# One decode step of a hybrid decoder: the sample tokens' experts move from the dense pass to gathered rows

## The chip, the cores and the metric

The kernel runs on one core of a Trainium2 chip. The metric is the device time of one execution in microseconds; the median of three runs is used. The engines are TensorE (PE, with its weight loads as PEld), VectorE (DVE), ScalarE (ACT), GpSimd (POOL) and SyncE (SP); 16 DMA engines serve all of them.

## What is computed

One layer works on 1024 prompt tokens and on 64 sample tokens (8 sequences of 8), each of 1024 channels. A state-space branch and a dilated attention branch are mixed, and a retrieval step over 16384 single-neuron experts follows. Only that last step is touched by the change:

```python
def block(xb):                       # 128 tokens
    q = einsum('td,dq->tq', xb, w_qp).reshape(TOKEN_BLOCK, PEER_HEADS, 2, PEER_HALF)
    s = einsum('thpe,hpke->thpk', q, sub_keys)
    sv, si = lax.top_k(s, PEER_TOPK)             # 16 of 128 keys, twice
    ...                                          # the 16 best pairs of each of 8 heads
    eidx = ...                                   # (128 tokens, 128 experts)
    gate = softmax(best, axis=-1).reshape(TOKEN_BLOCK, PEER_HEADS * PEER_TOPK)
    ue = jnp.take(u_tab, eidx, axis=0)
    act = gelu(einsum('td,tkd->tk', xb, ue))
    ve = jnp.take(v_tab, eidx, axis=0)
    return einsum('tk,tkd->td', gate * act, ve)
```

Each token so needs 128 of the 16384 rows of `u_tab` and of `v_tab`; a row has 1024 float32 values, 4 KB.

## The kernel before

The prompt is worked in two halves of 512 tokens. The 64 samples are projected with the first half (576 tokens there) and mixed with the second (576 tokens there). All large products are done in float32r in three parts (high times high, high times low, low times high).

The experts are worked in two ways. For the first half's 512 tokens, rows are gathered. `gather_u` (L1543) takes 128 tokens: for each of their 128 ranks one indirect DMA on POOL fetches 128 rows of `u_tab`, one per token (L1555), and DVE multiplies them with the tokens and sums (L1559). `gather_v` (L1574) takes a token at a time: one indirect DMA fetches the 128 rows of `v_tab` of that token (L1591), and PE sums them with the gates as weights, two tokens per group of eight `va` records (L1605). A row buffer holds 128 rows; there are eight (`RB`). That makes 512 gathers for u and 512 for v.

For the second half and the samples, 576 tokens, all 16384 experts are computed in a dense pass. `act` (L1401) works out the activations of 128 experts in two splits of 288 tokens: 48 matmuls, a piece that the trace shows as `tr`. `gates` (L1367) builds for each 128 tokens a table with the gate of every expert, zero where it wasn't chosen, four tokens at a time, and stores it in `G_scr`; this takes 144 groups of four tokens and 18 writes. `dense` (L1415) multiplies the activations by the gates and then by `v_tab`: `outs` (L1445) is a piece of 48 matmuls (`mm` in the trace), four for each group of four expert tiles, 128 in all; the last four are done in two halves of the tokens. Some pieces of `act` are done ahead as `early` (L1409), between the steps of choosing and `gates`, and wait in `A_scr`; there are 50 of them.

The gathers are spread over the work of the second half by a pacing scheme. Each piece of work calls `tick` (L89) with its cost in microseconds; `tick` multiplies it by a rate (`RATES`), and the generator `gather` (L1506) takes a step whenever enough has been collected. A step issues one gather and costs `RATE` = 1.9. `pace` sets the rate by stage: entries 0 and 1 for attention and the gated products of the second half, 5 and 6 up to the expert choice, 2 for the loop over the keys, 3 for choosing and gates, 4 for the dense pass. The letter beside a rate says whether u or v comes first if both can (with `None` they take turns); u may be up to three tiles of tokens ahead of v. `gemm_f` ticks 5.12 us for a piece, `outs` 2.9 us for each split. Work that was given out late is completed in `catch_up`. `after` makes each gather, each dot product and each `va` matmul come behind the last matmul that was emitted. What remains after the dense pass is drained (L331).

SP's queue loads all weights (L131, three buffers), and writes and reads `G_scr` and `A_scr`.

## Time and profile before

| | |
|---|---|
| median of three runs | 4129.87 us (4129.74 to 4141.28) |
| span of the profiled execution | 4130.7 us |
| PE / weight loads / DVE / ACT / POOL busy | 94 / 82 / 65 / 35 / 33% of the span |
| DMA | 1112.94 MB, mean 269 GB/s |
| choosing and gates of the second half | about 2050 to 2590 us |
| dense pass | about 2590 to 4100 us |

The span is the time from the first to the last instruction of one execution that the hardware profiler took; its stages can be told by the names of the tiles. A matmul's recorded duration has its way through the array in it and overlaps the next one's, so the price of a row of matmuls is read from their starts or from a whole piece, not from the mean duration. The DMA share is the mean busy share of the 16 DMA engines; as it is recorded it can pass 1 in a short stretch.

### The profile page before, as it was taken

Reading aid. Unit: us, or ns where it says so; the run is one execution under the profiler, and the core shown is the slowest. Engines: PE = TensorE matmul, PEld = TensorE weight load, DVE = VectorE, ACT = ScalarE, POOL = GpSimd, SP = SyncE. Lnnn points to the kernel's source line nnn. Section 1 sums busy time; section 2 is a strip of 40 time slices with the busy share of each in tenths; the row PEclk is TensorE's granted clock in tenths of the full one; section 3 lists DMA queues with packets and bytes.
Section 4 is the critical chain, followed back from the end, with each engine's and each line's share of the span. In section 5 each row is a group of like instructions: output and inputs, shape, how many; then the busy total and the mean of one; then the engine's idle time right before and its main releaser. Section 6 shows DMA issues by size and latency. Waiting matters only on the chain.

```text
span 4130.7 us, 74456 instructions
## 1 busy us (share of the span) xinstructions
PE 3897.4 (94%) x28935; PEld 3394.9 (82%) x28935; DVE 2681.5 (65%) x6776; ACT 1438.4 (35%) x2762; POOL 1349.3 (33%) x1236
## 2 busy tenths in 40 slices
PE   8899989899989967999999998999999999999997
PEld 8789964688878755987798998888888888898885
DVE  8627233556965868977897577566666666677554
ACT  3232233233233335212268897222222222222221
POOL 2620000000004335553311233455555554543334
PEclk9999999899999979999999999999999999999998
DMA  5575589444369789897756777999998999999998
GB/s 165 164 230 168 172 293 330 147 141 145 126 198 344 264 291 313 312 332 256 240 208 231 266 284 278 315 324 330 333 332 308 346 330 318 336 350 320 330 313 293
DMA packets 497985, 1112.94 MB, mean 269 GB/s; under 512 B 44752, under 2 KB 257104, under 8 KB 493792
## 3 DMA queue, kind: packets, MB, share of 16 engines
q1 hardware_dynamic: 350176, 571.26, 41.2%
q0 software_dynamic: 147456, 536.94, 35.9%
q8 instruction: 227, 3.72, 0.4%
q14 instruction: 126, 1.03, 0.1%
HBM read 991.77 MB, written 124.27 MB: 270 GB/s over the span
## 4 chain that ended last, share of the span: by engine, by line
PE 61%; DMA 4%; DVE 2%; ACT 1%; issue 1%; SPq 0%; POOL 0%; POOLq 0%; ACTq 0%; DVEq 0%
PE mm L77 34%; PE tr L77 20%; PE va L1605 6%; DMA V<-v_scr 1%; DVE row L1559 1%; DMA G<-G_scr 1%; DMA Q<-Q_scr 1%; DMA wraw<-in_w_out 1%; DMA row<-in_v_tab,eT 0%; ACT wH L133 0%; PE tr L953 0%; DVE wL L135 0%; ACT sm L935 0%; DMA kT<-k_scr 0%; ACT oij L1394 0%
## 5 line engine op out<-in xcount | busy, mean ns | idle before, releaser
L1555 POOL DMA_INDIRECT row<-in_u_tab,ei x512 | 664.9, 1299 | 1034.3 <-DVE row L1559 459.9
L133 ACT CAST wH<-wraw 128x1024 fp32r<-128x1024 f32 (+1 forms) x476 | 491.7, 1035 | 1330.3 <-PE mm L77 906.0
L135 DVE TENSOR_TENSOR wL<-wraw,wH 128x1024 fp32r<-128x1024 f32 (+1 forms) x476 | 578.6, 1216 | 521.5 <-ACT wH L133 457.5
L1591 POOL DMA_INDIRECT row<-in_v_tab,eT x512 | 570.8, 1115 | 911.6 <-PE va L1605 730.3
L77 PE MATMUL tr<-x2H,wH 128*128 128x288 f32 x2048 | 620.9, 303 | 13.1 <-ACT a L1406 11.0
L1559 DVE SCALAR_TENSOR_TENSOR row<-row,gxn 128x1024 f32<-128x1024 f32 x512 | 614.4, 1220 | 14.9 <-DMA row<-in_u_tab,ei 13.3
L77 PE MATMUL tr<-x2L,wH 128*128 128x288 f32 x2048 | 618.1, 302 | 0.0
L77 PE MATMUL tr<-x2H,wL 128*128 128x288 f32 x2048 | 617.3, 301 | 0.0
L77 PE MATMUL mm<-WH,wH 128*128 128x288 f32 (+2 forms) x2048 | 479.8, 297 | 0.4 <-ACT wH L133 0.2
L77 PE MATMUL mm<-WL,wH 128*128 128x288 f32 (+2 forms) x2048 | 479.8, 296 | 0.0
L77 PE MATMUL mm<-WH,wL 128*128 128x288 f32 (+2 forms) x2048 | 474.7, 296 | 0.0
L77 PEld LDWEIGHTS tr<-x2H,wH 128*128 128x128 f32 x2048 | 389.1, 190 | 38.1 <-issue 21.8
L77 PEld LDWEIGHTS tr<-x2H,wL 128*128 128x128 f32 x2048 | 389.1, 190 | 22.6 <-issue 21.8
L77 PEld LDWEIGHTS tr<-x2L,wH 128*128 128x128 f32 x2048 | 389.2, 190 | 21.0 <-issue 21.0
L77 PEld LDWEIGHTS mm<-WH,wH 128*128 128x128 f32 x2048 | 340.5, 188 | 39.2 <-issue 27.7
L77 PEld LDWEIGHTS mm<-WH,wL 128*128 128x128 f32 x2048 | 339.2, 188 | 33.5 <-issue 32.7
L77 PEld LDWEIGHTS mm<-WL,wH 128*128 128x128 f32 x2048 | 341.9, 188 | 27.7 <-issue 27.7
L77 PE MATMUL mm<-xnH,wH 128*128 128x288 f32 (+1 forms) x960 | 323.8, 337 | 0.0
L77 PE MATMUL mm<-xnL,wH 128*128 128x288 f32 (+1 forms) x960 | 320.5, 334 | 0.0
L77 PE MATMUL mm<-xnH,wL 128*128 128x288 f32 (+1 forms) x960 | 320.4, 334 | 0.0
L1461 DVE TENSOR_TENSOR acc<-acc,mm 128x288 f32<-128x288 f32 (+2 forms) x496 | 204.9, 450 | 172.4 <-PE mm L77 138.8
L1605 PE MATMUL va<-row,strips 128*32 128x512 f32 x2048 | 279.5, 616 | 12.0 <-DMA row<-in_v_tab,eT 12.0
(387 smaller groups left out, 7487.6 us busy)
## 6 DMA issues: line engine op xcount, KB each, us to landing
wraw<-in_v_tab SPq DMA_DIRECT2D x132, 512.0 KB
wraw<-in_uT SPq DMA_DIRECT2D x128, 512.0 KB
G_scr<-Gt SPq DMA_DIRECT2D x18, 2048.0 KB
G<-G_scr SPq DMA_DIRECT2D x32, 1152.0 KB
cc<-in_kc SPq DMA_DIRECT2D x48, 512.0 KB
cc<-in_vc SPq DMA_DIRECT2D x48, 512.0 KB
wraw<-in_w_g SPq DMA_DIRECT2D x32, 512.0 KB
wraw<-in_w_qp SPq DMA_DIRECT2D x32, 512.0 KB
```

Of the source, the lines that this page charges most:

```text
L77: self.last = self.nc.tensor.matmul(out, lhsT=lhsT, rhs=rhs, **kw)
L133: nc.scalar.copy(h, raw)
L135: nc.vector.tensor_sub(l, raw, h.bitcast(F32))
L1461: v.tensor_add(o, o, ps[:, :c1 - c0])
L1555: self.after(nc.gpsimd.indirect_dma_start(out=row, out_offset=None, in_=a["u_tab"], in_offset=bass.IndirectOffsetOnAxis(ap=ei[:, k:k + 1], ...
L1559: self.after(v.scalar_tensor_tensor(row, row, 1.0, xn, op0=ALU.mult, op1=ALU.mult, accum_out=act[:, k:k + 1]))
L1591: self.after(nc.gpsimd.indirect_dma_start(out=row, out_offset=None, in_=a["v_tab"], in_offset=bass.IndirectOffsetOnAxis(ap=eT[:, tk:tk + 1 ...
L1605: self.after(nc.tensor.matmul(va[0][c:c + 32, :], lhsT=self.strips[:, s, j, 31 - t:63 - t], rhs=rows[j][:, b * 512:(b + 1) * 512], start=t ...
```

## The change

The dense pass keeps the second half's 512 tokens alone. Every matmul of `act` and `outs` then has one split of 512 columns, 24 matmuls per piece; `G_scr`, `A_scr` and the tiles of the pass shrink from 576 to 512 tokens, and `gates` and the output step no longer run for the samples. The samples' experts are still chosen with the second half, as its fifth tile; `pack_samples` then copies their gates and expert numbers by four small DMAs so that 64 tokens times two halves of the ranks fill 128 partitions, and `gather` takes them as a fifth tile of tokens: 64 gathers for u, 64 for v. `ranks_first` stands in for the transpose, since the packed tile has another shape. The rates of the key loop (0.6 to 0.8), of choosing and gates (0.5 to 1.0) and of the dense pass (1.149 to 1.21) rise, and `outs` ticks 0.01 us per token instead of 2.9 us per split. The normed samples are written to `xn2_scr` for the gathers. Comments are gone too; hunks of comments alone are left out here.

```diff
-RATES = ((0.9, 'u'), (1.3, 'u'), (0.6, 'v'), (0.5, 'v'), (1.149, None), (0.6, 'v'), (0.3, 'v'))
+RATES = ((0.9, 'u'), (1.3, 'u'), (0.8, 'v'), (1.0, 'v'), (1.21, None), (0.6, 'v'), (0.3, 'v'))
...
-            self.x2, self.xn2 = d("x2_scr", [1088, D]), d("xn2_scr", [512, D])
+            self.x2, self.xn2 = d("x2_scr", [1088, D]), d("xn2_scr", [576, D])
...
-            self.Gd, self.Ad = d("G_scr", [18, 128, 128, 32]), d("A_scr", [56, 128, 576])
+            self.Gd, self.Ad = d("G_scr", [16, 128, 128, 32]), d("A_scr", [56, 128, 512])
...
-                if h == 0:
-                    nc.sync.dma_start(self.xn2[r0:r0 + rows], xn)
+                if h == 0 or i == 4:
+                    nc.sync.dma_start(self.xn2[min(r0, 512):min(r0, 512) + rows], xn)
...
-                    if h:
-                        self.gates(kg, i, rows, lambda: self.early(da, x))
+                    if h and i < 4:
+                        self.gates(kg, i, lambda: self.early(da, x))
+                    elif h:
+                        self.pack_samples()
...
+    def pack_samples(self):
+        out = []
+        for n, x in zip(("gs", "es"), self.peer[1, 4]):
+            t = self.gp.tile([128, 64], F32, name=n)
+            for kh in range(2):
+                self.nc.sync.dma_start(t[kh * 64:kh * 64 + 64], x[:64, kh * 64:kh * 64 + 64])
+            out.append(t)
+        self.peer[0, 4] = tuple(out)
...
-        t = da.tile([128, 576], F32, name="a", tag="a", bufs=AB)
-        for ps, (c0, c1) in zip(self.gemm_f(a["uT"][i], x, SPLITS[576], get=self.trt), SPLITS[576]):
+        t = da.tile([128, 512], F32, name="a", tag="a", bufs=AB)
+        for ps, (c0, c1) in zip(self.gemm_f(a["uT"][i], x, SPLITS[512], get=self.trt), SPLITS[512]):
...
-                G[0] = dn.tile([128, 18, 4, 32], F32, name="G", tag="G", bufs=2)
+                G[0] = dn.tile([128, 16, 4, 32], F32, name="G", tag="G", bufs=2)
...
-            W[i] = [dn.tile([128, 576], F32R, name="W" + n, tag="W" + n, bufs=6) for n in "HL"]
+            W[i] = [dn.tile([128, 512], F32R, name="W" + n, tag="W" + n, bufs=6) for n in "HL"]
...
-        def outs(r, dq, splits=SPLITS[576]):
+        def outs(r, dq, splits=SPLITS[512]):
...
-            self.tick(2.9 * len(splits))
+            self.tick(0.01 * sum(c1 - c0 for c0, c1 in splits))
...
-        for c0, c1, tiles in ((256, 576, (2, 3, 4)), (0, 256, (0, 1))):
+        for c0, c1, tiles in ((256, 512, (2, 3)), (0, 256, (0, 1))):
...
-        us, ws = [self.gather_u(i) for i in range(4)], [self.gather_v(i) for i in range(4)]
+        us, ws = [self.gather_u(i) for i in range(5)], [self.gather_v(i) for i in range(5)]
...
-        while nv < 4:
-            can = [nu < 4 and nu < nv + 3, nv < nu]
+        while nv < 5:
+            can = [(0, nu) in self.peer and nu < nv + 3, nv < nu]
             pick = {"u": 0, "v": 1}.get(self.want, turn // 2 % 2)
             turn += 1
+            if not any(can):
+                yield RATE
+                continue
...
+    def ranks_first(self, x):
+        nc = self.nc
+        ps = self.trt()
+        if x.shape[1] == 128:
+            nc.tensor.transpose(ps[:, :128], x, self.ident)
+            return ps[:, :128]
+        for kh in range(2):
+            r = slice(kh * 64, kh * 64 + 64)
+            nc.tensor.matmul(ps[r, :64], lhsT=x[r], rhs=self.ident[r, r], start=True, stop=True)
+        return ps[:, :64]
...
+        n = 128 if i < 4 else 64
         xn = gp.tile([128, D], F32, name="gxn", tag="gxn", bufs=1)
-        nc.sync.dma_start(xn, self.xn2[i * 128:(i + 1) * 128])
+        for r in range(0, 128, n):
+            nc.sync.dma_start(xn[r:r + n], self.xn2[i * 128:i * 128 + n])
...
-        for k in range(128):
+        for k in range(n):
...
-        for hf in range(2):
+        for hf in range(n // 64):
...
-                nc.sync.dma_start(a["yp"][r0:r0 + 64], x3)
+                nc.sync.dma_start(a["yp"][r0:r0 + 64] if i < 4 else a["ys"], x3)
```

## Rows read from the trace of the kernel before

**Rows 1.** The page: busy us, share of the span and instructions by engine.

```profile
PE 3897.4 (94%) x28935; PEld 3394.9 (82%) x28935; DVE 2681.5 (65%) x6776; ACT 1438.4 (35%) x2762; POOL 1349.3 (33%) x1236
```

**Rows 2.** Stretches: length, busy us (count) PE PEld DVE ACT POOL, clock, DMA share, GB/s.

```profile
2050.00:2590.00 540.00, 519.77 (x4014) 490.95 (x4013) 398.40 (x902) 423.08 (x907) 139.25 (x101) 0.98 0.69 253
2600.00:3640.00 1040.00, 1037.91 (x7714) 922.61 (x7715) 670.34 (x1201) 252.17 (x367) 547.38 (x460) 1.00 0.94 328
...
2600.00:4130.00 1530.00, 1506.75 (x11156) 1310.29 (x11156) 976.48 (x1871) 359.12 (x501) 735.23 (x632) 0.99 0.93 325
```

**Rows 3.** The chain that ended last: start, us, what; first half, then dense pass.

```profile
1228.54 5.60 PE mm L77 x24
...
3149.91 6.34 PE mm L77 x48
```

**Rows 4.** Groups by line: tile, count, busy us, mean ns, idle before.

```profile
L77 PE MATMUL mm<-oij 128*128 128x128 f32 x1152 | 175.2, 276 | 0.1
...
L1559 DVE SCALAR_TENSOR_TENSOR row<-row,gxn 128x1024 f32<-128x1024 f32 x512 | 614.4, 1220 | 14.9 <-DMA row<-in_u_tab,ei 13.3
...
L1461 DVE TENSOR_TENSOR acc<-acc,mm 128x288 f32<-128x288 f32 (+2 forms) x496 | 204.9, 450 | 172.4 <-PE mm L77 138.8
...
L1501 DVE TENSOR_TENSOR G<-G,mm 128x512 f32<-128x512 f32 (+1 forms) x10 | 6.3, 679 | 0.0
```

**Rows 5.** PE in order of time around one group of `va`: start, us, what.

```profile
3200.80 0.29 PE L77 MATMUL tr<-x2H,wH 128*128 128x288 f32 x1
3200.93 0.29 PE L77 MATMUL tr<-x2L,wH 128*128 128x288 f32 x1
3201.15 1.07 PE L1605 MATMUL va<-row,strips 128*32 128x512 f32 x8
...
3202.39 0.29 PE L77 MATMUL tr<-x2H,wH 128*128 128x288 f32 x1
```

**Rows 6.** POOL and ACT groups up to 2600 us, then POOL from 2600 us.

```profile
L1555 POOL DMA_INDIRECT row<-in_u_tab,ei x260 | 358.7, 1380 | 773.2 <-DVE row L1559 412.8 <-DMA out_kvp<-kt 198.4 <-DVE stat L932 55.4
L1591 POOL DMA_INDIRECT row<-in_v_tab,eT x132 | 141.7, 1073 | 386.9 <-PE va L1605 341.7 <-issue 18.9 <-DVE row L1559 12.8
...
L1406 ACT ACTIVATE a<-tr 128x288 f32<-128x288 f32 x111 | 45.7, 412 | 36.5 <-PE tr L77 35.5 <-issue 0.7
...
L1591 POOL DMA_INDIRECT row<-in_v_tab,eT x380 | 429.1, 1129 | 524.7 <-PE va L1605 388.6 <-issue 68.1 <-DVE row L1559 37.4
```

**Rows 7.** Choosing: its last step on DVE (min/median/max ns, first to last start); a stretch there.

```profile
L1353 DVE TENSOR_REDUCE ef<-df x72: 274/604/987, 1109.6 to 2225.7; 128x16 f32<-128x128 uint32 x16, 128x16 f32<-128x320 uint32 x16, 128x16 f32<-128x560 uint32 x16, 128x16 f32<-128x800 uint32 x16
...
2100.00:2200.00 100.00, 98.97 (x770) 93.80 (x768) 94.43 (x341) 85.55 (x184) 9.55 (x8) 1.00 0.52 191
```

**Rows 8.** The page's DMA queues (packets, MB, share of 16 engines) and issues.

```profile
q1 hardware_dynamic: 350176, 571.26, 41.2%
q0 software_dynamic: 147456, 536.94, 35.9%
...
G_scr<-Gt SPq DMA_DIRECT2D x18, 2048.0 KB
G<-G_scr SPq DMA_DIRECT2D x32, 1152.0 KB
```

**Rows 9.** Stretches with the highest DMA share or GB/s.

```profile
3800.00:3900.00 100.00, 100.00 (x742) 83.97 (x741) 57.60 (x118) 20.60 (x26) 38.75 (x37) 1.00 0.98 342
...
3500.00:3525.00 25.00, 25.00 (x190) 22.90 (x187) 16.24 (x29) 5.33 (x7) 11.70 (x13) 1.00 1.04 392
...
1700.00:1800.00 100.00, 95.93 (x719) 94.61 (x718) 90.73 (x151) 24.30 (x36) 58.50 (x46) 1.00 0.96 352
```

**Rows 10.** POOL's v gathers from 3700 to 4100 us.

```profile
L1591 POOL DMA_INDIRECT row<-in_v_tab,eT x134 | 144.7, 1080 | 241.3 <-PE va L1605 212.1 <-issue 19.5 <-ACT spare L197 7.0
```

**Rows 11.** The end: PE in order of time (start, us, what, idle before); a stretch.

```profile
4104.76 1.94 PE L1605 MATMUL va<-row,strips 128*32 128x512 f32 x8 [2.54 <-DMA row<-in_v_tab,eT]
...
4100.00:4125.00 25.00, 11.39 (x48) 1.40 (x48) 12.08 (x55) 4.03 (x7) 4.61 (x5) 0.57 0.76 286
```

More of the change, by code (lines that the diff above doesn't have):

```diff
@@ L1364, in choose, with gates @@
         self.peer[h, i] = (gf, ef)
-    def gates(self, kp, i, rows, between):
+    def pack_samples(self):
[6 more added lines that the diff above has]
+        self.peer[0, 4] = tuple(out)
+    def gates(self, kp, i, between):
         nc = self.nc
@@ L1371, in gates @@
         gf, ef = self.peer[1, i]
-        R = rows
+        R = 128
         e = kp.tile([128, 2, 128], I32, name="e", tag="e", bufs=1)[:R]
@@ L1419, in dense @@
         A, W, G = {}, {}, {}
-        acc = dn.tile([128, 8, 576], F32, name="acc")
+        acc = dn.tile([128, 8, 512], F32, name="acc")
         def scores(i):
@@ L1426, in scores @@
             if i in self.ahd:
-                A[i] = da.tile([128, 576], F32, name="a", tag="a", bufs=AB)
+                A[i] = da.tile([128, 512], F32, name="a", tag="a", bufs=AB)
                 nc.sync.dma_start(A[i], self.Ad[127 - i])
@@ L1439, in weights @@
             t = A.pop(i)
-            tv = t.rearrange("p (b t) -> p b t", b=18)
+            tv = t.rearrange("p (b t) -> p b t", b=16)
             v.tensor_mul(tv, tv, G[0][:, :, i % 4, :])
-            W[i] = [dn.tile([128, 576], F32R, name="W" + n, tag="W" + n, bufs=6) for n in "HL"]
+            W[i] = [dn.tile([128, 512], F32R, name="W" + n, tag="W" + n, bufs=6) for n in "HL"]
             self.split(W[i][0], W[i][1], t)
-        def outs(r, dq, splits=SPLITS[576]):
+        def outs(r, dq, splits=SPLITS[512]):
             h, l = self.load_piece(vt[:, r * 4:r * 4 + 4, dq * 256:(dq + 1) * 256], view=4)
@@ L1480, in dense @@
         for _ in range(2):
-            t = dn.tile([128, 18, 4, 32], F32, name="G", tag="G", bufs=2).rearrange("p b i t -> p (b i t)")
+            t = dn.tile([128, 16, 4, 32], F32, name="G", tag="G", bufs=2).rearrange("p b i t -> p (b i t)")
             space += [t[:, :D], t[:, D:2 * D]]
@@ L1492, in dense_out @@
         nc, a = self.nc, self.a
-        R = 128 if i < 4 else 64
         r0 = 512 + i * 128
-        x3 = x3[:R]
-        nc.sync.dma_start(x3, self.x2[r0:r0 + R])
+        nc.sync.dma_start(x3, self.x2[r0:r0 + 128])
         for b in range(2):
@@ L1499, in dense_out @@
             for k in range(4):
-                nc.tensor.transpose(ps[:R, k * 128:(k + 1) * 128], acc[:, b * 4 + k, i * 128:i * 128 + R], self.ident)
-            nc.vector.tensor_add(x3[:, b * 512:(b + 1) * 512], x3[:, b * 512:(b + 1) * 512], ps[:R])
-        self.rms(pool, x3, g, acc[:, :, min(i, 3) * 128:min(i, 3) * 128 + 128])
-        nc.sync.dma_start(a["yp"][r0:r0 + R] if i < 4 else a["ys"], x3)
+                nc.tensor.transpose(ps[:, k * 128:(k + 1) * 128], acc[:, b * 4 + k, i * 128:i * 128 + 128], self.ident)
+            nc.vector.tensor_add(x3[:, b * 512:(b + 1) * 512], x3[:, b * 512:(b + 1) * 512], ps)
+        self.rms(pool, x3, g, acc[:, :, i * 128:i * 128 + 128])
+        nc.sync.dma_start(a["yp"][r0:r0 + 128], x3)
     def gather(self):
@@ L1546, in gather_u @@
         gf, ef = self.peer[0, i]
+        n = 128 if i < 4 else 64
         xn = gp.tile([128, D], F32, name="gxn", tag="gxn", bufs=1)
-        nc.sync.dma_start(xn, self.xn2[i * 128:(i + 1) * 128])
-        ei = gp.tile([128, 128], I32, name="ei", tag="ei", bufs=1)
+        for r in range(0, 128, n):
+            nc.sync.dma_start(xn[r:r + n], self.xn2[i * 128:i * 128 + n])
+        ei = gp.tile([128, 128], I32, name="ei", tag="ei", bufs=1)[:, :n]
         v.tensor_copy(ei, ef)
-        act = gp.tile([128, 128], F32, name="act", tag="act", bufs=2)
-        for k in range(128):
+        act = gp.tile([128, 128], F32, name="act", tag="act", bufs=2)[:, :n]
+        for k in range(n):
             row = gp.tile([128, D], F32, name="row", tag="row", bufs=RB)
@@ L1566, in weights @@
             v.tensor_mul(act, act, gf)
-            ps = self.trt()
-            nc.tensor.transpose(ps[:, :128], act, self.ident)
-            self.gw[i] = gp.tile([128, 128], F32, name="wT", tag="wT", bufs=3)
-            v.tensor_copy(self.gw[i], ps[:, :128])
+            ps = self.ranks_first(act)
+            self.gw[i] = gp.tile([128, 128], F32, name="wT", tag="wT", bufs=3)[:, :n]
+            v.tensor_copy(self.gw[i], ps)
         self.wait[i] = [GL, weights]
@@ L1576, in gather_v @@
         v = nc.vector
-        ps = self.trt()
-        nc.tensor.transpose(ps[:, :128], self.peer[0, i][1], self.ident)
-        eT = gp.tile([128, 128], I32, name="eT", tag="eT", bufs=2)
-        v.tensor_copy(eT, ps[:, :128])
-        for hf in range(2):
+        n = 128 if i < 4 else 64
+        eT = gp.tile([128, 128], I32, name="eT", tag="eT", bufs=2)[:, :n]
+        v.tensor_copy(eT, self.ranks_first(self.peer[0, i][1]))
+        for hf in range(n // 64):
             va = []
@@ L1612, in outs @@
             def outs(hf=hf, va=va):
-                r0 = i * 128 + hf * 64
+                r0 = i * 128 + hf * 64 if i < 4 else 1024
                 x3 = gp.tile([128, D], F32, name="x3", tag="row", bufs=RB)[:64]
```

## The prediction

> **What bounds the kernel now.** I read the page's busy shares first [rows 1]: TensorE (PE) is busy for 94% of the span, VectorE (DVE) 65%, ScalarE 35%, GpSimd (POOL) 33%. The stretches [rows 2] tell by stage, with the DMA engines beside them. From 2050 to 2590 us, where the experts of the second half are chosen and the gates are built, PE is 96% busy and the DMA engines 69%. From 2600 us on, in the dense pass over all experts, PE is busy 99.8% of the time up to 3640 us, and DMA 94%. The chain of waits [rows 3] agrees: in the dense pass it is a row of PE pieces of 48 matmuls. So PE sets the time now, with the DMA engines some 5% behind it. A change that takes PE work out of the dense pass and puts gathers in meets the second limit at once, and most of what follows is about how much of the first gain the second one lets through.
>
> **The change part by part. PE, matmul pieces.** A piece of the dense pass for 576 tokens is 48 matmuls of 288 columns and takes 6.34 us; a piece for 512 tokens exists already in the first half, 24 matmuls of 512 columns in 5.60 us [rows 3]. The change turns all 256 pieces (128 of `act`, 128 of `outs`, the last four of these in two halves) from the first into the second: 256 x 0.74 = -189 us of PE. 50 pieces of `act` lie ahead of the dense pass as `early` work now, 48 afterwards, since `gates` of the fifth tile and its two calls of `early` go.
>
> **PE, gates.** 144 groups of four tokens take 175.2 us of PE [rows 4], 1.22 us each; 16 groups go: -20 us.
>
> **PE, gathered rows.** The samples add 64 gathers for the products with u and 64 for those with v. Two v gathers feed one group of eight `va` matmul records. The matmuls around one such group start every 0.13 us, as at 3200.80 and 3200.93; the second after it starts at 3202.39 where 3201.19 was due [rows 5]. So a group costs PE 1.20 us, and 32 new groups +38 us. PE's sum over the kernel is -189 - 20 + 38 = -171 us.
>
> **The other engines.** DVE gets 64 dot products of 1.22 us (+78 us) [rows 4] and 32 small copies, and loses the gates' 16 comparisons and half the additions into `acc` (four of 0.45 us per piece become two of about 0.68 us, as the 512-column additions at the end, -53 us [rows 4]); at 64% in the dense pass that is covered. POOL gets 128 gathers of 1.1 to 1.4 us and is busy for 48% of the dense pass [rows 2, 6]. Both cost nothing unless DVE rises by a third. `pack_samples` adds four small DMAs on SP's queue that wait for the fifth tile's gates; behind them stand weight loads. The last of the `choose` work ends at 2226 us [rows 7], and these DMAs come after the gates of tile 3, the last step ahead of the dense pass, so I take the wait as zero; without that cover it would be the fifth tile's look-up of its indices, 8 times two steps of 0.6 us [rows 7], 10 us; it can't be a gain, since the DMAs are only added. `ranks_first` is two matmuls instead of a transpose, below 1 us.
>
> **DMA.** The gather queue is busy 35.9% of 16 engines for 1024 gathers [rows 8]: 1.448 us of all 16 engines for one gather of 0.524 MB. The other queue needs 41.2% of the span for 571 MB, 2.98 us per MB. The change adds 128 x 1.448 = +185 us and takes away about 12.7 MB (two of the 18 writes of gates and a ninth of the reads [rows 8], and the `A_scr` pieces, 50 of 295 KB each way that become 48 of 262 KB), -38 us. So DMA work grows by 147 us while PE work falls by 171.
>
> **Where the gathers go.** Each `tick` hands out its microseconds times the rate, and a gather costs 1.9. By the calls, the key loop hands out 188 us of ticks (16 x 11.12 + 2 x 5.12): 59 gathers at 0.6, 79 at 0.8. Choosing and gates hand out 336 us now (48 x 5.12 + 18 x 5): 88 gathers at 0.5; afterwards 316 us, 166 gathers at 1.0. Together +98 ahead of the dense pass. The dense pass hands out 1142 us now (690 gathers), 1065 us afterwards (678). At 2600 us 392 are issued (260 u, 132 v) and 632 are left [rows 6]; afterwards about 489 are issued, of them 233 v (tile 0's 128, then the second u tile's rest, then v again, as `can` allows), and 663 are left. So 31 more are left for the dense pass, not 128.
>
> **Ahead of the dense pass:** PE 50 x 6.34 -> 48 x 5.60 is -48 us, gates -20, and 50 more `va` groups +61: -7 us. DMA there has room: 540 us at 0.69 is 373 us busy, and 78 gathers at 1.448 less the gates' and `A_scr` writes make it about 465 of 533 us, 87%. I take -7; the bounds are -25 (the groups fall into gaps; PE has 20 us of idle time there) and +25 (the groups queue behind choosing, where DVE is 94% busy [rows 7]).
>
> **The dense pass:** 55.5 of the 128 `act` pieces are done at 2600 us (111 activations of half a piece [rows 6]), so PE has 72.5 of them and 128 of `outs` after it, and two more afterwards: 200.5 x 6.34 = 1271 us against 202.5 x 5.60 = 1134, -137. Of v gathers 380 are left now [rows 6], 343 afterwards: 18 groups less, -22 us. PE alone would so end the 1530 us in 1371. DMA: 0.93 x 1530 = 1423 us busy now [rows 2]; +31 x 1.448 = +45, gates and `A_scr` reads and the samples' rows -17: 1451 us. That is more than PE's 1371. The bound changes hands: **the dense pass becomes as long as its DMA work over the share that the DMA engines can hold.** That share isn't shown at its limit. The nearest rows: 0.97, 0.98 and 0.98 in three successive stretches of 100 us from 3600 us, the last of which stands here, without any PE idle time, so the limit is not below 0.977; single stretches of 25 us read 1.02 to 1.06, nine of them after 2700 us; one stands here with 1.04 [rows 9], so it may lie above 1 as it is recorded. I take 0.99, nearer to the long stretches: 1451 / 0.99 = 1466 us, -64. The bounds: 1.06 gives 1369 and so PE's 1371 (-159), 0.93 as now gives 1560 (+30).
>
> Sum: 4130.7 - 7 - 64 = 4060 us. The profiled span of 4130.7 lies 0.8 us above the median 4129.87, so this is also the forecast of the median.
>
> **The rivals.** *PE stays the bound.* If the DMA engines carry 508 MB (325 GB/s x 1530 us, plus 31 gathers, less 6 MB) in PE's 1371 us, 371 GB/s, the whole gain comes through: 4131 - 7 - 159 = 3965. For it: a stretch of 25 us at 392 GB/s. Against it: the best 100 us anywhere shows 352 GB/s at a share of 0.96 [rows 9]. The Trainium skill, HBM Reference, Specifications, says that a core streaming alone measures about 425 GB/s; by that rule 371 would fit and this rival would be the result. No stretch of this trace shows 425; its own rows at best bear out 392 for 25 us, so I give it a quarter.
>
> *The gathers fall behind, and the end is a tail of gathers* (slower). The rows live in eight buffers, so a gather waits until an earlier one is used. Late in the pass the ticks of `outs` hand out 3.5 gathers per piece (5.8 x 1.149 / 1.9), and a piece with 1.75 `va` groups costs PE 8.4 us: 41 gathers per 100 us. From 3700 to 4100 us, where nearly all gathers are for v, 134 of these are issued, 34 per 100 us, and POOL waits 212 us for `va` [rows 10]: gathers lag already. If they lag from the start of the dense pass, at the DMA share of 0.93 that the pass has now, PE's matmuls end early, and what is left runs alone: `va` groups at 1.94 us instead of 1.07, after PE sat idle for 2.5 us for its rows, with the granted clock at a mean of 0.57 [rows 5, 11], near the lower of its two levels (1.2 and 2.4 GHz). 1451 / 0.93 = 1560 us: +30, and 4131 - 7 + 30 = 4154. It decides against the change from a mean share below 0.948 (1451 / 1530).
>
> *Nothing measurable*: the share settles between 0.94 and 0.955, within 0.3% (12 us) of the time before, about the least that a measurement of this kernel can tell from no change. That the new pacing doesn't do what it says belongs here too: were the 98 gathers not issued ahead, they would be 142 us more of DMA work in the dense pass, (1451 + 142) / 0.99 = 1609, +79, against 68 us saved ahead of it without their `va` groups: 4142.
>
> **How the numbers follow.** Forecast, DMA-bound at a share of 0.96 to 1.02 (4025 to 4112): 0.42. PE-bound or nearly (3950 to 4025): 0.25. No change (4118 to 4142): 0.13. Slower by lag or tail (4142 to 4200): 0.20. So faster by over 0.3% 0.67, same 0.13, slower 0.20. The range leaves out about 0.1 at either end: 3965, the PE-bound time, to 4155, the tail's.
>
> **What would show it.** Right: `tr` and `mm` pieces of 24 matmuls in 5.6 us throughout; about 490 gathers issued when the dense pass starts; DMA share 0.97 or more over the dense pass; PE no longer 100% busy there, or a tail of some tens of gathers after the last `outs`. PE-bound would show as PE at 99% with over 365 GB/s. Wrong: a DMA share that stays at 0.93 to 0.95, `va` rows waiting long after the last matmul piece, or a stretch from 2050 to 2600 that has become longer, with SP waiting at `pack_samples` or PE at `strips`.

## The result and the profile after

The changed kernel takes 4222.83 us (median of four runs, 4215.64 to 4229.27) against 4129.81 us for the kernel before beside it: 1.0221 times as long, 95% interval 1.0201 to 1.0240. I had forecast 4060 us in a range of 3965 to 4155. The direction was wrong, and the time lies outside the range. The profiled execution has a span of 4227.2 us, 96.5 us more than before.

The page of the changed kernel: the line of the engines, then the two large DMA queues (packets, MB, share of 16 engines). They answer to [rows 1] and [rows 8].

```profile
PE 3773.6 (89%) x23012; PEld 2918.2 (69%) x23012; DVE 2695.6 (64%) x6672; ACT 1370.2 (32%) x2555; POOL 1505.8 (36%) x1364
...
q1 hardware_dynamic: 341760, 559.66, 40.2%
q0 software_dynamic: 165888, 604.05, 39.3%
```

PE went from 94% busy to 89% of a longer span, so it is no longer the engine that is always at work. To see where the time went I cut both executions at the same two events: the last `Gt` that the gates write (the end of choosing and gates), and the last addition into `acc` (the end of the dense pass). What follows is the tail of gathers. The stretches of before (columns as in [rows 2]):

```profile
1850.00:2564.40 714.40, 702.61 (x5369) 634.21 (x5366) 534.14 (x1685) 464.91 (x979) 199.09 (x160) 0.99 0.70 251
2564.40:4094.00 1529.60, 1506.98 (x11160) 1321.89 (x11159) 981.25 (x1843) 360.61 (x503) 739.75 (x633) 0.99 0.94 327
4094.00:4130.70 36.70, 15.19 (x80) 3.12 (x78) 14.48 (x62) 4.03 (x7) 8.45 (x9) 0.63 0.72 269
```

And of after, cut at the same events:

```profile
1850.00:2628.50 778.50, 723.50 (x4249) 547.86 (x4249) 539.76 (x1745) 424.76 (x852) 287.00 (x238) 0.96 0.78 278
2628.50:4101.00 1472.50, 1315.61 (x6153) 929.25 (x6153) 983.96 (x1635) 332.86 (x422) 752.01 (x627) 0.94 0.95 332
4101.00:4227.20 126.20, 65.26 (x312) 9.57 (x310) 22.78 (x108) 5.54 (x10) 65.50 (x68) 0.61 0.86 316
```

Choosing and gates end 64 us later. The dense pass is 57 us shorter, and the tail is 89.5 us longer. 64 - 57 + 89.5 is the 96.5 us. PE's busy time in the dense pass fell by 191 us, yet the pass became only 57 us shorter: PE now stands idle for 157 of its 1472 us. The waits of PE in the changed kernel (engine, line, released by, us in total, times, longest), first from 2123.7 to 2628.5 us:

```profile
PE mm L77 <- ACT oij L1406: 30.1, 25, 2.9
PE tr L77 <- ACT a L1418: 8.6, 7, 3.5
```

and then in the dense pass:

```profile
PE tr L1561 <- DVE act L1594: 75.7, 2, 74.4
PE va L1631 <- DMA row<-in_v_tab,eT: 49.0, 13, 9.3
```

In the kernel before, PE's only listed wait in choosing and gates (2110.2 to 2564.4 us) is this one:

```profile
PE tr L77 <- ACT a L1406: 2.9, 2, 2.2
```

In its dense pass (2564.4 to 4094 us) a transpose behind a tile's dot products waited too, but for 15.2 us, and no `va` group is listed:

```profile
PE tr L1568 <- DVE act L1566: 15.2, 1, 15.2
```

So there are new waits in two places: for the gates' comparisons (`oij`) ahead of the dense pass, and for gathered rows in it.

### The profile page after: what moved, and what is told of

The parts are those of the page before. It is cut to its first block, busy times and chain, and to the rows that moved or that the text cites. A ratio compares the mean times of both kernels' runs of the same rounds, so it can differ in the third digit from the quotient of the medians.

```text
span 4227.2 us, 62685 instructions
## 1 busy us (share of the span) xinstructions
PE 3773.6 (89%) x23012; PEld 2918.2 (69%) x23012; DVE 2695.6 (64%) x6672; ACT 1370.2 (32%) x2555; POOL 1505.8 (36%) x1364
## 4 chain that ended last, share of the span: by engine, by line
PE 67%; DMA 9%; DVE 9%; issue 7%; POOL 5%; ACT 2%; SPq 1%; POOLq 0%; another core or an unknown queue 0%; DVEq 0%; ACTq 0%
PE mm L77 42%; PE tr L77 17%; PE va L1631 6%; POOL row L1583 3%; DMA row<-in_v_tab,eT 2%; DVE wL L135 1%; DVE row L1587 1%; DMA row<-in_u_tab,ei 1%; DMA cc<-in_kc 1%; POOL row L1617 1%; DMA Q<-Q_scr 1%; DMA G<-G_scr 1%; DMA wraw<-in_w_out 1%; ACT wH L133 0%; DVE qz L1096 0%
## 5 line engine op out<-in xcount | busy, mean ns | idle before, releaser
L77 PE MATMUL mm<-WH,wH 128*128 128x512 f32 (+1 forms) x1056 | 410.9, 390 | 18.4 <-ACT WH L185 13.4
L77 PE MATMUL tr<-x2H,wH 128*128 128x512 f32 x1024 | 415.1, 405 | 11.8 <-ACT a L1418 8.6
L77 PE MATMUL mm<-WH,wL 128*128 128x512 f32 (+1 forms) x1056 | 408.9, 392 | 10.2 <-DVE wL L135 10.2
L77 PE MATMUL tr<-x2H,wL 128*128 128x512 f32 x1024 | 412.9, 403 | 0.0
L77 PE MATMUL tr<-x2L,wH 128*128 128x512 f32 x1024 | 411.8, 402 | 0.0
L77 PE MATMUL mm<-WL,wH 128*128 128x512 f32 (+1 forms) x1056 | 409.7, 388 | 0.0
L1473 DVE TENSOR_TENSOR acc<-acc,mm 128x512 f32<-128x512 f32 (+1 forms) x256 | 169.8, 669 | 136.1 <-PE mm L77 131.8
L77 PEld LDWEIGHTS tr<-x2H,wH 128*128 128x128 f32 x1024 | 195.5, 191 | 77.6 <-issue 17.6
L77 PEld LDWEIGHTS tr<-x2H,wL 128*128 128x128 f32 x1024 | 194.9, 190 | 68.5 <-issue 24.3
L77 PEld LDWEIGHTS mm<-WL,wH 128*128 128x128 f32 x1056 | 199.1, 189 | 56.4 <-issue 15.9
```

Source lines behind the costliest of these rows:

```text
L77: self.last = self.nc.tensor.matmul(out, lhsT=lhsT, rhs=rhs, **kw)
L1473: v.tensor_add(o, o, ps[:, :c1 - c0])
```

## Two views of the new waits

VectorE's queue in the changed kernel, in order of time (start, us, what), in the middle of the gates:

```profile
2268.56 1.22 DVE L1403 TENSOR_TENSOR oij<-i,T 128x1024 f32<-128x1024 f32 x1
2269.70 1.22 DVE L1587 SCALAR_TENSOR_TENSOR row<-row,gxn 128x1024 f32<-128x1024 f32 x1
...
2270.84 1.22 DVE L1403 TENSOR_TENSOR oij<-i,T 128x1024 f32<-128x1024 f32 x1
2271.98 1.22 DVE L1587 SCALAR_TENSOR_TENSOR row<-row,gxn 128x1024 f32<-128x1024 f32 x1
...
2273.12 1.22 DVE L1587 SCALAR_TENSOR_TENSOR row<-row,gxn 128x1024 f32<-128x1024 f32 x1
...
2274.27 1.22 DVE L1403 TENSOR_TENSOR oij<-i,T 128x1024 f32<-128x1024 f32 x1
```

and PE at the same time; the last line is the same row of eight matmuls 160 us later:

```profile
2270.27 2.07 PE L77 MATMUL mm<-oij 128*128 128x128 f32 x8 [1.79 <-ACT oij L1406]
2273.67 2.07 PE L77 MATMUL mm<-oij 128*128 128x128 f32 x8 [1.33 <-ACT oij L1406]
...
2436.33 1.05 PE L77 MATMUL mm<-oij 128*128 128x128 f32 x8
```

One or two dot products of 1.22 us stand between every two comparisons of the gates (a comparison goes from DVE through a scaling on ACT, which the wait names, to PE). PE's eight matmuls of a group come after a wait of 1.3 to 1.8 us and then take 2.07 us instead of 1.05. In the 100 us from 2240 us PE's granted clock is 0.79 in the mean, between its two levels (1.00 is 2.4 GHz, 0.50 is 1.2 GHz); in the 100 us from 2400 us, where PE has no such gaps, it is 1.00.

The other view is the 74 us. PE in order of time in the dense pass:

```profile
2969.71 0.39 PE L77 MATMUL mm<-WH,wL 128*128 128x512 f32 x1
3044.54 0.47 PE L1561 MATMUL tr<-ident,act 128*128 128x128 f32 x1 [74.44 <-DVE act L1594]
3044.67 0.78 PE L77 MATMUL tr<-x2H,wH 128*128 128x512 f32 x1
3045.24 0.63 PE L77 MATMUL tr<-x2L,wH 128*128 128x512 f32 x1
```

The faster rates had brought v level with u (v 256, u 309 of a tile that ends at 384, counted from POOL's gathers up to 2900 us). The next v products need the transposed weights of the third u tile, and the transpose that makes them stands in PE's queue ahead of the next piece of `act`. From 2900 us on 75 u gathers must land and be multiplied before it can run; at 1.448 us each these are 109 us of DMA work. The transpose reaches the head of the queue at 2970 us and stands there until 3044 us.

PE's queue isn't the only one that stands still. SP's queue, which loads all weights, has the load of the next u tile's tokens (`gxn`, one buffer) in it, and waits for the last dot product of the old tile (SP's waits from 2628 to 3110 us):

```profile
SPq L1576 <- DVE row L1587: 70.3, 1, 70.3
```

No weight load starts between 2973 and 3055 us. With three buffers for weights, PE could have worked three pieces of 5.6 us at most in the gap (an estimate) if the transpose had not stood ahead of them. So the place of the transpose alone hardly explains the 74 us; a run that moves only one of the two was not made.

## The experiments

Two theories stand behind the expectations. *Order*: the place of gathers, dot products and `va` groups in the engines' queues costs the time. *DMA*: the work of the DMA engines sets the length of dense pass and tail. Each run was made beside the kernel before.

The rates and the samples, apart. *after_old_rates* takes back the pacing alone:

```diff
-RATES = ((0.9, 'u'), (1.3, 'u'), (0.8, 'v'), (1.0, 'v'), (1.21, None), (0.6, 'v'), (0.3, 'v'))
+RATES = ((0.9, 'u'), (1.3, 'u'), (0.6, 'v'), (0.5, 'v'), (1.149, None), (0.6, 'v'), (0.3, 'v'))
```

> The changed kernel with the rates of before (0.6, 0.5, 1.149). Counting the ticks, 376 gathers are handed out ahead of the dense pass and some 644 in it, so that 130 or more are left for a tail. Theory order: gates end before 2565 us (PE has 68 us less to do there), no stall on the transposes, matmuls end near 3960 to 4000, then a tail of 130 to 180 v gathers at 1.56 us (as the 64 of the changed kernel's tail took): 4190 to 4270. Theory DMA: the dense pass with its tail is 1531 us of DMA work plus 98 x 1.45 = 142 at a share of 0.95, from 2510 us on: 4270.

Measured: 4245.57 us, ratio 1.0283 (1.0263 to 1.0304). The stretches, as above:

```profile
1850.00:2550.50 700.50, 660.55 (x3858) 522.77 (x3856) 496.79 (x1620) 413.16 (x841) 168.72 (x142) 0.97 0.66 233
2550.50:3933.60 1383.10, 1299.85 (x6069) 931.57 (x6073) 960.54 (x1590) 333.95 (x423) 695.04 (x583) 0.97 0.96 336
3933.60:4242.50 308.90, 149.66 (x692) 19.50 (x684) 85.46 (x257) 7.64 (x14) 200.51 (x204) 0.59 0.95 364
```

The last `Gt` is back at 2550 us, and the dense pass is 146 us shorter than before, but the 204 gathers that are left over make a tail of 309 us. The samples' gathers found no room. The time lies in the order theory's range and 25 us below the 4270 of the DMA theory.

*before_new_rates* gives the old kernel the new rates and nothing else (the same line, the other way round).

> The kernel before with the new rates alone (0.8, 1.0, 1.21); dense pass for 576 tokens, no sample gathers. Theory order: the faster v-first rates alone make v catch up with u; PE waits on the transpose of a tile's weights appear and the gates end later than 2565; slower than before by 30 to 120 us although no work is added. Theory DMA: the work is the same and 98 gathers have moved to a stretch where the DMA share was 0.69, so the dense pass is relieved: same or faster, 4080 to 4135.

Measured: 4217.16 us, ratio 1.0221 (1.0200 to 1.0241), with no sample gathered and no tile changed. The last `Gt` comes at 2649 us, 84 us late, and the same wait has appeared (2120 to 2649 us):

```profile
PE mm L77 <- ACT oij L1394: 24.2, 14, 8.5
```

The remaining stretch is 1562 us, against 1566 before. 100 gathers fewer are issued in it (542 against 642), but its dense pass has PE busy for 1480 of 1541 us at a DMA share of 0.86: PE sets the length, so fewer gathers bring nothing. No work was added and 87 us were lost, as the order theory said (30 to 120 us slower); the DMA theory (same or faster) fails here.

*no_samples* takes the fifth tile out of `gather`, at the new rates:

```diff
-                        self.pack_samples()
+                        self.nc.sync.dma_start(self.a["ys"][:, :128], self.peer[1, 4][0][:64])
...
-        us, ws = [self.gather_u(i) for i in range(5)], [self.gather_v(i) for i in range(5)]
+        us, ws = [self.gather_u(i) for i in range(4)], [self.gather_v(i) for i in range(4)]
...
-        while nv < 5:
-            can = [(0, nu) in self.peer and nu < nv + 3, nv < nu]
+        while nv < 4:
+            can = [nu < 4 and nu < nv + 3, nv < nu]
```

> The changed kernel without the 128 gathers of the samples: their rows are not summed, and the output for the sample tokens is only filled with other data; rates as in the changed kernel, so the other 1024 gathers are issued earlier than before the change. It prices the dense pass at 512 tokens by itself. Theory order: v still catches up with u, so stalls at the same two places and in the gates remain (about 150 us of PE), but no tail of gathers: 4050 to 4110. Theory DMA: 128 x 1.45 = 186 us of DMA work less, all of it off the end: 4223 - 186 = 4037, with PE's idle time in the dense pass gone, 4000 to 4050. PE's sum alone would give 4130.7 - 209 = 3920.

Measured: 4106.02 us, ratio 0.9942 (0.9926 to 0.9959); the last `Gt` at 2628 us as in the changed kernel, a tail of 20 us. The dense pass:

```profile
2627.90:4090.20 1462.30, 1316.95 (x6187) 929.88 (x6187) 916.90 (x1523) 336.04 (x424) 657.43 (x566) 0.94 0.90 313
```

It is 10 us shorter than the changed kernel's at a DMA share of 0.90 instead of 0.95: with less DMA work the waits of PE's queue (the same gap, 73 us here, and 41 us for rows) set its length. That is the order theory's case.

*no_samples_old_rates* joins this edit with the line of the old rates; what is left of the change is 512 tokens for 576 in the dense pass and gates.

> The changed kernel with the rates of before and without the samples' 128 gathers: their dot products, va groups and result rows are left out, and the samples' output is filled with other data. What is left is the dense pass at 512 tokens against 576, at the same number of gathers as before. PE theory (256 pieces are 0.74 us cheaper and nothing else is in the way): last Gt near 2550 us, matmuls of the dense pass done near 3940, and at most some 76 v gathers after it: 3990 to 4070 us. DMA theory (1024 gathers don't fit in the shorter pass, the gathers' own lag sets the end): 4070 to 4130 us, with a tail of 100 us or more.

Measured: 4076.93 us, ratio 0.9877 (0.9853 to 0.9901), in the band of the DMA theory, with its tail of over 100 us:

```profile
2553.60:3941.10 1387.50, 1307.55 (x6146) 929.54 (x6149) 936.36 (x1552) 333.78 (x423) 688.62 (x580) 0.97 0.96 335
3941.10:4072.90 131.80, 67.51 (x352) 10.46 (x351) 25.25 (x114) 5.65 (x10) 74.05 (x77) 0.69 0.90 339
```

Together the medians make a table:

| | rates of before | rates of after |
|---|---|---|
| 576 tokens in the dense pass | 4129.87 | 4217.16 |
| 512 tokens, samples left out | 4076.93 | 4106.02 |
| 512 tokens, samples gathered | 4245.57 | 4222.83 |

At the old rates the smaller pass brings 53 us of the 209 that PE saves (189 + 20), and the samples' gathers cost 169 us of the 185 us of DMA work that they are. The new rates cost 87 us on the old kernel and 29 without the samples; with them they gain 23, since more of the left-over gathers are done early. The change is -53 + 169 - 23 = +93 us.

*lead_none*: the letter of choosing and gates, `RATES[3] = (1.0, None)` for `(1.0, 'v')`, so that v does not run level with u.

> The changed kernel with one edit: while the second half's experts are chosen and its gates built, u and v take turns (None) instead of v first. Counting the ticks, the dense pass then begins with u about one tile of tokens ahead of v (some 300 u, 172 v) instead of 256 and about 220, so that v never catches up with the tile of u that it needs. Theory order (v catches up with u, the rest of the u tile comes in one burst, and PE's transpose of that tile's weights stands at the head of PE's queue until the burst is through): the wait of 74 us on that transpose goes and the stall around 3500 us too; gates end near 2580 us instead of 2629; 4223 falls to 4090 to 4140. Theory DMA (the pass is as long as its DMA work, whatever the order): PE's waits only move, 4190 to 4230. If the order matters in the dense pass alone: about 4130 to 4160.

Measured: 4195.07 us, ratio 1.0169 (1.0148 to 1.0190), in the DMA theory's band. The gap of 74 us is gone, and others have taken its place (PE's waits in the dense pass, 2615.2 to 4060.4 us; the last `Gt` comes at 2615 us, not near 2580):

```profile
PE va L1631 <- DMA row<-in_v_tab,eT: 55.0, 17, 6.7
PE va L1631 <- DVE row L1587: 30.0, 9, 4.4
```

The next runs ask what makes choosing and gates longer. *u_early* changes the letters of `RATES[5]` and `RATES[6]` to `'u'`, *key_loop_only* sets `RATES[3]` back to 0.5.

> The changed kernel with the letters of RATES[5] and RATES[6] (the stages ahead of the key loop) 'u' instead of 'v'; the rates themselves stay. So as many gathers are asked for ahead of the dense pass, but the second tile of tokens' u rows come before choosing begins and none among choosing and gates. Theory A (the stage of gates is longer because 48 dot products of 1.22 us stand in DVE's queue between the gates' own comparisons of 1.22 us, for which PE waits): no dot product falls between 2150 and 2550 us, PE's waits for oij fall from 30 us to under 12, the last Gt is written at 2565 to 2595 us instead of 2628, and as u is further ahead of v when the dense pass starts, PE's wait of 74 us for the transposed weights goes too: 4090 to 4150 us in all. Rival B (the number of gathers and va groups ahead of the dense pass makes the stage long, in whatever order): the last Gt stays within 10 us of 2628, and the whole is 4140 to 4230 us, the change coming from the dense pass alone.

> The changed kernel with RATES[3] back at 0.5; the faster key loop (0.8) and dense pass (1.21) stay. Theory A (dot products among the gates lengthen the stage): the last Gt at 2560 to 2590 us, with fewer than 35 dot products between 2150 and 2550 us; some 60 gathers more than in the changed kernel are left for the dense pass, so the tail after the last addition into acc grows from 126 to 180 to 260 us, and the whole is 4200 to 4250 us. Rival (the key loop's rate already does the harm): the last Gt at 2610 to 2640 us.

*u_early* gave 4239.33 us, ratio 1.0264 (1.0236 to 1.0293), the last `Gt` at 2646 us. *key_loop_only* gave 4226.30 us, ratio 1.0244 (1.0214 to 1.0273), the last `Gt` at 2542 us and a tail of 275 us. Neither did what it was meant to: u had come only from 208 to 228 when the key loop began, so 28 dot products were still among the gates, and with the slower rate 44 of the 48 were. Both keep waits for `oij` of 25 and 33 us. 2542 us isn't to be compared with 2628 either, since 47 pieces of `act` were done by then instead of 55. They don't price the dot products, but they show that the wait doesn't go by their number: 28 of them cost nearly the wait of 48. In *u_early* the transpose of a tile's weights also stands at the head of PE's queue among the gates, longer than the 7.3 us of the changed kernel:

```profile
PE tr L1561 <- DVE act L1594: 25.1, 1, 25.1
```

*no_dots_in_gates* gets the second u tile done ahead of the gates, at the same rates:

```diff
-RATES = ((0.9, 'u'), (1.3, 'u'), (0.8, 'v'), (1.0, 'v'), (1.21, None), (0.6, 'v'), (0.3, 'v'))
+RATES = ((0.9, 'u'), (1.3, 'u'), (0.8, None), (1.0, 'v'), (1.21, None), (0.6, 'u'), (0.3, 'u'))
```

> The changed kernel with other letters alone: RATES[5] and RATES[6] 'u', RATES[2] None (u and v by turns in the key loop), the rates themselves as changed. u_early and key_loop_only still had 28 and 48 dot products among the gates, so neither told what these cost; here the second u tile is done ahead of the first gate. Theory A (dot products ahead of the gates' comparisons on DVE make PE wait for oij): PE's waits for oij fall from 30 us to 17 or less, the stretch 2240 to 2340 us no longer shows PE at 70% with a clock of 0.79, and the last Gt, at the same 55 pieces of act, comes at 2580 to 2605 us instead of 2628. Theory B (only the number of va groups counts): the last Gt within 10 us of 2628. Either way the DMA engines still limit what follows (some 1500 us of DMA work at a share of 0.945): 4170 to 4210 us under A, 4205 to 4235 us under B.

Measured: 4173.28 us, ratio 1.0108 (1.0081 to 1.0135). The stretch from 2240 us, first in the changed kernel and then here:

```profile
2240.00:2340.00 100.00, 70.21 (x344) 60.26 (x344) 91.71 (x126) 77.87 (x178) 65.35 (x42) 0.79 0.90 326
```

```profile
2240.00:2340.00 100.00, 99.27 (x590) 71.01 (x590) 45.83 (x59) 71.34 (x152) 40.41 (x34) 1.00 0.85 313
```

DVE falls from 92% to 46%, PE rises from 70% to 99% and its clock from 0.79 to 1.00. ACT is busy for 78 and 71%. PE's wait for `oij` in the whole stage is 4.8 us (30.1 in the changed kernel), the transpose's wait of 7.3 us is gone with the dot products, and the last `Gt` comes at 2598 us with the same 55 pieces done. Theory A holds for these 30 us, and by letters alone the changed kernel's loss of 93 us is about halved (30 us ahead of the last `Gt`, 26 behind it). Also 128 v gathers stand in this stage, more than the changed kernel's 82; so the number of `va` groups is not what cost those 30 us.

Now the dense pass and the tail. *u_early_faster* is *u_early* with `RATES[4]` 1.4 for 1.21.

> As u_early, with RATES[4] (the dense pass) 1.4 instead of 1.21, so that all gathers are asked for before the last piece of outs. If the tail costs more than the same gathers among matmuls: the tail falls from some 120 us to under 40 us, the pass before it grows by less, and the whole is 20 to 50 us below u_early. If the DMA engines are the limit of dense pass and tail together: within 15 us of u_early, with the DMA share of the dense pass at 0.96 or more. If PE's queue is the limit (a va group or a transpose at its head holds the matmuls behind it): as slow as u_early or slower, with more of PE's waits put down to va and to the transposes.

Measured: 4239.10 us, ratio 1.0267 (1.0245 to 1.0289), the same as *u_early*. The tail fell from 122 to 51 us, the pass grew from 1470 to 1543 us, the sum is 1594 us against 1592, and the DMA share of the pass 0.95 in both. Where the last gathers stand makes no difference to the time. This run doesn't tell DMA and order apart: the time is that of both, the share of 0.96 that the DMA theory asked for was missed, and PE's waits in the pass grew as the order theory said, for the transposes from 71.9 to 106.0 us and for v rows from 49.4 to 73.0 us.

*half_v_weights* takes 33.5 MB of DMA work out and leaves every engine its instructions:

```diff
+        if view == 4:
+            nc.sync.dma_start(raw[:, :n // 2].rearrange("p (a b) -> p a b", a=2), src[:, :2])
+            raw = raw[:, :n // 2].unsqueeze(1).to_broadcast([128, 2, n // 2])
...
```

> The changed kernel, with each of the 128 weight pieces of outs loaded by half: 256 KB come from the table and the splits on ACT and DVE read that half twice, so every engine does as many instructions of the same size as before and only 33.5 MB of DMA work is gone, 100 us of all 16 engines at 2.98 us per MB. The result of the dense pass is so computed with wrong weights. DMA theory (dense pass and tail together are as long as their DMA work over a share of some 0.945): the stretch from the last Gt to the end falls from 1599 to 1480 to 1515 us, the tail from 126 to under 60 us, and the whole is 4105 to 4145 us. Order theory (PE's queue, held by va groups and transposes whose rows or products are late, sets the length, and the DMA engines could do more): the stretch stays within 25 us of 1599, with the DMA share down to 0.88 or so: 4195 to 4230 us.

Measured: 4141.28 us, ratio 1.0022 (1.0008 to 1.0036). The stretches after the last `Gt`, which comes at 2627 us as in the changed kernel:

```profile
2627.40:4066.80 1439.40, 1330.63 (x6275) 932.30 (x6279) 986.95 (x1667) 336.55 (x425) 787.04 (x658) 0.96 0.94 327
4066.80:4140.70 73.90, 37.89 (x192) 6.33 (x192) 16.99 (x76) 3.92 (x7) 35.40 (x37) 0.63 0.83 317
```

Of the 100 us of DMA work (by the page the hardware queue needs 0.387 x 4140.7 = 1602 us instead of 1699), 86 come back: 1513 us instead of 1599. PE has no less to do; its waits have become shorter (the gap of 74 us is 52 us, the waits for v rows in the pass fall from 49 to 25 us). The DMA theory holds for this stretch (its tail of under 60 us was missed, it is 74).

*more_ahead*: *no_dots_in_gates* with `RATES[0]` 1.1, `RATES[1]` 1.5, `RATES[2]` 0.9.

> As no_dots_in_gates, with RATES[0] 1.1 for 0.9, RATES[1] 1.5 for 1.3 and RATES[2] 0.9 for 0.8, so some 50 gathers more come between 1300 and 2100 us, where the DMA engines have a share of 0.65 to 0.9 and PE is idle for up to a fifth of the time. DMA theory: 50 gathers fewer from 2600 us on are 72 us of DMA work, 76 us less of dense pass and tail, against 0 to 30 us that the earlier stages become longer (DVE is 70 to 90% busy there with 1.22 us per dot product): 4100 to 4165 us. If the earlier stages pay as much as the dense pass gains (each gather costs some 1.5 us wherever it is put): 4165 to 4215 us. Faster than the kernel before (under 4117) would need the whole gain and no price.

Measured: 4166.71 us, ratio 1.0088 (1.0058 to 1.0117). 34 gathers fewer are left at the last `Gt` (661 against 695) and dense pass and tail are 41 us shorter, but the last `Gt` comes 33 us later. A gather costs nearly as much ahead of the dense pass as it frees in it. No version that gathers the samples beat the kernel before.

*six_buffers*: *no_dots_in_gates* with `RB = 6`.

> no_dots_in_gates with six row buffers instead of eight (RB = 6); more than eight don't fit in memory. POOL waits for a buffer to come free before most gathers of the dense pass, and the DMA share there is 0.96. If the eight buffers are what keeps the DMA engines from a higher share (a gather can't be asked for until an earlier row is used), two fewer cost a quarter of what can be under way: the share of the dense pass falls to 0.92 or less, dense pass and tail grow from 1573 to over 1610 us, and the whole is 4210 us or more. If the DMA engines are full and the wait for a buffer only shows it: the stretch stays within 20 us of 1573, the whole within 4160 to 4200 us.

Measured: 4266.46 us, ratio 1.0325 (1.0295 to 1.0355). The whole fits the buffer theory, the share doesn't: the DMA share of the dense pass is 0.95 (0.96 with eight, and 0.92 or less was expected) and the pass takes 1462 us (1456). It issues 612 gathers there instead of 631, so the buffers cost the pass a little as well. What grows most is the stage ahead, by 25 us, and the tail, from 117 to 168 us, with 85 gathers for 64 and a lower share:

```profile
4085.10:4253.00 167.90, 85.68 (x376) 11.73 (x376) 25.50 (x117) 5.65 (x10) 81.21 (x85) 0.54 0.84 294
```

So fewer buffers cost the gathers that run alone far more than the dense pass. Whether more than eight would help wasn't tried.

The stretch from the last `Gt` to the end in seven of the kernels (share: mean of dense pass and tail by their lengths):

| kernel | last `Gt` | us from there to the end | gathers in it | DMA share |
|---|---|---|---|---|
| before | 2564 | 1566 | 642 | 0.935 |
| after | 2629 | 1599 | 695 | 0.943 |
| after_old_rates | 2551 | 1692 | 787 | 0.958 |
| no_samples_old_rates | 2554 | 1519 | 657 | 0.955 |
| no_dots_in_gates | 2598 | 1573 | 695 | 0.953 |
| half_v_weights | 2627 | 1513 | 695 | 0.935 |
| more_ahead | 2631 | 1532 | 661 | 0.944 |

## Why the prediction was wrong

**What held.** The bound did pass from PE to the DMA engines in the dense pass: PE is idle there for 157 us, and *half_v_weights* gains from DMA work alone. Its pieces cost what was forecast; two lines of the chain of waits of after, beside [rows 3]:

```profile
3155.63 5.50 PE mm L77 x24
...
3174.60 5.59 PE tr L77 x24
```

No wait of note is put down to `pack_samples` (3.4 us in SP's queue): its DMAs for the gates are issued at 2377 us, 250 us ahead of the last `Gt`, and not behind the gates of tile 3, where I had placed them.

**The step "ahead of the dense pass: -7 us", with bounds of -25 and +25, failed.** It is +64. The sum was made of PE's work alone, and the other engines were passed with their mean shares ("both cost nothing unless DVE rises by a third"). I had named "the groups queue behind choosing, where DVE is 94% busy" for the bound [rows 7] and thought of `va` groups there. But the rate of 1.0 finishes v's first tile earlier, and then hands out u: 48 dot products among the gates' comparisons, on an engine that every group goes through ahead of PE. The kernel before has dot products among its gates too, 38 from 2365 to 2562 us, one in 5.2 us, and no listed wait for `oij`; the changed kernel has its 48 from 2245 to 2348 us, one in 2.1 us. So their number alone doesn't make the wait. How close they stand, and how much other work PE has meanwhile, is the likely reason; the two were not tried apart (at the old rates 25 of them beside the shorter pieces come with a wait of 17 us).

*no_dots_in_gates* brings back 30 of the 64 us. For the rest only the account is shown. *after_old_rates* gains 14 us ahead of the pass, not the 68 that I counted (48 + 20); PE waits 17 us for `oij` there and 15 for ACT's `a`. Against that run the changed kernel writes its first `Gt` 25 us later (2098.3 and 2123.7 us), and its gates take 53 us more, in which `va` groups keep PE busy for 44 us instead of 23; the 30 us are part of these 53. What makes the 25 us was not tried. The tally also gave 489 gathers at 2600 us, and 451 were there.

**The step "1451 / 0.99 = 1466 us" failed in its share, and a little in its work.** I took 0.99 from the best stretches of 100 and of 25 us [rows 9]. No kernel here holds that share over the whole: 0.935 to 0.958 in the table. From the last `Gt` to the end the forecast came to 1566 - 64 = 1502 us, which at 0.99 stands for 1487 us of DMA work. Measured are 1599 us. The work in them is 0.95 x 1472.5 + 0.86 x 126.2 = 1507 us: 695 gathers were left at the last `Gt`, where I had counted 663 at 2600 us. At 0.99 this work would take 1523 us, 21 us more than forecast; the other 76 us are the share of 0.943. With the 71 us ahead of the pass these 97 are the whole miss. The queues of the page tell the same: the gathers' queue grew by 0.393 x 4227.2 - 0.359 x 4130.7 = 178 us, as forecast (185), while the other one, with 12 MB less, still needs 1699 us against 1702. I had counted -38 there at a fixed price per MB; it was 2.98 us before and is 3.04 now. The samples' gathers aren't what raised it: without them it is 0.415 x 4110.6 / 558.54 = 3.05 us in *no_samples*, and 3.02 in *before_new_rates*, with the bytes of before.

**The rival of the tail was the right one, and its price was right for its place.** It said that a mean share below 0.948 decides against the change, that dense pass and tail would take 30 us more at 0.93, and that the end would be `va` groups at 1.94 us that wait for rows. The share is 0.943 and the stretch 32 us longer. That the 30 us were so well met is in part luck: there were 1507 us of DMA work instead of 1487, and a share of 0.943 instead of 0.93, and these two errors cancel. The end of after, PE in order of time, beside [rows 11]:

```profile
4131.80 1.94 PE L1631 MATMUL va<-row,strips 128*32 128x512 f32 x8 [3.15 <-DMA row<-in_v_tab,eT]
4135.11 1.94 PE L1631 MATMUL va<-row,strips 128*32 128x512 f32 x8 [1.37 <-DMA row<-in_v_tab,eT]
```

With +64 us in place of its -7 the rival would have said 4154 + 71 = 4225. I gave it 0.20, since I weighed the highest short stretches against it, when the mean of the whole pass in the trace of before, 0.93 [rows 2], was the value to stay with.

**What I had not seen at all** is the gap of 74 us, in which one u tile held the queues of PE and SP. In the changed kernel it costs little by itself: the DMA engines work through it (a share of 0.93 from 2900 to 3100 us), and *no_dots_in_gates*, with a gap of 74.6 us, needs 1573 us from the last `Gt` on, *lead_none*, without one and with 694 gathers, 1565. Where the DMA engines have less to do, as in *no_samples*, it sets the length.

**What stays open**: why dense pass and tail settle between 0.935 and 0.96 and not above. With two buffers fewer the share of the pass went from 0.96 to 0.95 only, so the buffers aren't shown to be the reason. Nor is the DMA work told apart everywhere from the order of the queues: most of PE's waits in the pass end with gathered rows or their products.

## What to carry to other kernels

Where the bound passes from one engine to a resource that is some 5% behind it, divide the work by the mean share that the resource has held over a whole stage, not by its best stretches, and expect moved work to pay its full price there: 128 gathers of 1.448 us cost 169 of 185 us. Before a rate is raised, ask what the scheme will hand out once its first choice runs out, and lay that work against the engine that the stage waits for, in that stretch; 48 dot products of 1.22 us, packed between the gates' comparisons, lost 30 us ahead of the dense pass; done ahead of the first gate they lost none of it, and the first `Gt` came no later (2122.7 us against 2123.7).

## What the runs showed of the hardware

The DMA engines can move more bytes a second than they do in the dense pass. With the gathers nearly alone, in the tail of *after_old_rates*, single stretches of 25 us read like this (columns as in [rows 2]):

```profile
4000.00:4025.00 25.00, 8.50 (x40) 1.11 (x40) 13.18 (x25) 0.00 (x0) 19.21 (x20) 0.50 1.02 409
4025.00:4050.00 25.00, 10.14 (x48) 1.46 (x43) 11.38 (x24) 0.84 (x2) 15.99 (x17) 0.50 1.03 385
4050.00:4075.00 25.00, 12.57 (x60) 1.70 (x64) 5.96 (x25) 1.15 (x2) 15.50 (x16) 0.61 0.89 312
```

The first reads 409 GB/s at a share of 1.02, and 10.21 of its 10.22 MB are gathers. The whole tail moves 364 GB/s at a share of 0.95, against 332 GB/s at 0.95 in the changed kernel's dense pass: 10% more for the same share, when gathers of 4 KB rows run with hardly any weight loads beside them. A rate in GB/s is so that of one mix of transfers, and not of another. The Trainium skill, HBM Reference, Specifications, states about 425 GB/s for a core that streams alone. No run here shows that: the highest stretches of 25 us read 412 GB/s (*half_v_weights* from 4075 us, *key_loop_only* from 3975 us). In the kernel before it is 397 from 1700 us, a little above the 392 that the prediction's rival of PE went by.

The clock follows PE's gaps: 0.79 where PE waited for `oij` in the gates and over 2900 to 3100 us with the 74 us gap, 0.61 in the tail, and 0.50, the lower of its two levels, in the first of the stretches above, where PE is busy for 8.5 of 25 us. The matmuls right behind the gap take 0.63 us each by the record, and 0.39 ahead of it.
